# A two-layer encoder on one Trainium2 core: merged vector operations, another order of products, and another end of the last norm

## The chip, the core and the metric

The kernel runs on one core of one Trainium2 chip. Each engine has an instruction queue of its own: TensorE (PE) multiplies, VectorE (DVE), ScalarE (ACT) and GpSimd (POOL) work on rows, SyncE (SP) issues DMAs, and POOL issues some as well. The metric is the device time of one execution in microseconds. Before, the median of three runs is 1638.21 us, from 1637.58 to 1638.83.

## The reference

A trunk of two layers over 512 tokens of width 1024, all in float32. Each layer is

```python
proj = x @ w_in[i]          # q, k, v of attention; q, k, v, g of retention; two gates
ya = neighbourhood_attention(...)   # 8 heads of 64, window 8 x 16 on a 64-wide grid
yb = bidirectional_retention(...)   # 4 heads, key width 128, value width 256
merged = sigmoid(gate_a) * (ya @ w_branch_a[i]) + sigmoid(gate_b) * (yb @ w_branch_b[i])
x = layer_norm(ALPHA * x + merged @ w_out[i], ln1_g[i], ln1_b[i])
ffn = conv_glu_ffn(x, w_up[i], conv_w[i], conv_b[i], w_down[i])
ple = sigmoid(x @ w_ple_gate[i]) * (p[i] @ w_ple_proj[i])
x = layer_norm(ALPHA * x + ffn + ple, ln2_g[i], ln2_b[i])
```

`conv_glu_ffn` makes two halves of width 2816, convolves each over three neighbouring tokens, forms gelu(a) * b and multiplies by `w_down`. The output is the 512 x 1024 array after the second layer.

## The kernel before

**Numbers.** Each float32 operand of a product is held as a rounded part and a remainder: `hi` is made by ACT, `lo = raw - hi` by DVE (128x1024 per weight tile, line 842 `split`). One product is then three matmuls, high by high, high by low and low by high (`mm3`, line 1179). Large products go over 2x2 blocks with seven block products in place of eight, called `a`, `c`, `t1`, `t2`, `d`, `t3`, `t4`. Five of them take sums or differences of blocks as operands. For the down-projection these come from `s_sums` (line 2156) out of the gated halves `gg`, in four DVE instructions of 256 columns, and are then split into `sh` and `sl`.

**Tokens.** Token rows lie in four tiles of 128. `R[0]` to `R[3]` are the running sums of the output tiles; `N1` and `N2` are their column halves of 512. `into` (line 2292, and another after line 2409) adds a product from PSUM to a half of R, `stats` takes mean and variance of it (`bn`), `moments` joins these in `mv`. `rstd` is the inverse deviation, made on POOL from a `ve` of ACT.

**Order.** Nothing is issued when it is written down. `Program` records every operation (so all rows have the one line L278), and a list scheduler (`_order` line 563, `_best` line 494) puts each region in order by due times and rough costs; `_best` repeats this for `ROUNDS` rounds with random shifts from `SEED` and keeps the best. The order of PE's products within a region comes from tables: `VG` and `FILL` for the projections, the heads (R0 to R3 retention, N0 to N7 attention) and the blocks 2 to 9 between them, `PG` for the gate products, `UP_ORDER` for the up-projection of each layer in two parts (`0a` is block product `a` of unit 0, `g` the product with the embedding gate, `A0` to `A3` the affine step of the first norm of one tile, `s` a down sum), and `SUMS_AT` for the places of some sums. The last part of the last layer (plan 0) is issued as written.

**Retention head.** `qk` are the rotated queries and keys, `s` their products, `wx` the decay weights, `ta = s * wx`, `kz` the weighted keys, from which PE makes the state `st`.

**Affine step.** The first norm's output for the residual needs four multiplications of `xn` by a half of the gain (`lnh`) and two additions to R per tile.

**End.** The last block product, `t4`, is made for tile 2 and then for tile 3, 24 matmuls of 512 columns each. For each tile: add, `bn`, `mv`, then the norm. Tile 1 goes out by a DMA of POOL that adds to the bias, which an SP DMA has put into the output far earlier. Tile 0 gets gain and shift from POOL and goes out by SP. Tile 2's scaling by `rstd` is done by ACT, its shift by POOL, per half. Tile 3 is done by DVE alone: times the gain `gp`, then `rstd` and the shift `bp2`. `gp` and `bp2` are copies of gain and shift in PSUM, in halves. Inside these, the writes are

```python
def norm_b(t, R=R):
    shift_0(slice(768, 1024))
    nc.sync.dma_start(out[:P, :], R[0])
    for c in (N1, N2):
        nc.scalar.activation(R[t][:, c], R[t][:, c], AF.Copy, scale=rs[t])
        nc.gpsimd.tensor_add(R[t][:, c], R[t][:, c], b2c[:, c])
        nc.sync.dma_start(out[t * P:(t + 1) * P, c], R[t][:, c])
```

## Time and profile before

| | |
|---|---|
| median of three runs | 1638.21 us |
| profiled execution | 1637.16 us |
| its span in the trace | 1635.4 us |
| granted TensorE clock, as a share of full speed | 0.999 |
| instructions in the trace | 26401 |
| HBM traffic over the span | 327.37 MB read, 27.79 MB written |

The profile shows one execution. The span is what the trace holds from first to last instruction; the rest of the 1637.16 us lies around it. Busy time is the union of an engine's instructions. In a timeline row stand start, duration, engine, line, operation, output and inputs, and in brackets how long the engine had waited ahead of it and for whom. In a row of groups stand count, busy time, mean nanoseconds of one, and idle time ahead of them. PE's matmuls overlap a little in the records: one of 256 columns is recorded with 283 ns, and 24 in a row take 2.88 us.

### The profile page before, as it was taken

To read this page: it belongs to the slowest core of one execution; us is meant where nothing else is said; L and a number is where in the kernel's file an instruction comes from. 1 tells how busy PE (TensorE), PEld (TensorE's weight loads), DVE (VectorE), ACT (ScalarE), POOL (GpSimd) and SP (SyncE) were. 2 spreads that over 40 slices of the span, in tenths; PEclk is the share of its full clock that TensorE was granted. 3 is DMA by queue.
4 is the path that set the end of the run, shared out by engine and by line. 5 is a ranking of instruction groups with operands and counts; after the bars stand their busy time and mean duration, and the time that the engine had idled before them with its cause. 6 is when DMAs were issued, how large, how long until landed. Compare 5 with 4: busy or idle time off the path is not lost.

```text
span 1635.4 us, 26401 instructions
## 1 busy us (share of the span) xinstructions
PE 1622.0 (99%) x10005; PEld 1460.9 (89%) x10005; DVE 1390.4 (85%) x2122; ACT 1027.0 (63%) x1545; POOL 246.3 (15%) x296
## 2 busy tenths in 40 slices
PE   9999999999999999999999999999999999999997
PEld 7889999888889899899888999998888998998986
DVE  6756998678978999879998779986799699997788
ACT  6664868645577667457486458785456675574554
POOL 0210211101211112101111111210012111110113
PEclk9999999999999999999999999999999999999999
DMA  8996777868798888769687977688598988788675
GB/s 308 269 237 164 172 153 200 273 207 252 197 290 227 224 262 203 224 211 222 174 263 190 285 186 185 176 225 251 191 261 224 283 238 238 206 204 271 175 169 129
DMA packets 108032, 360.57 MB, mean 220 GB/s; under 512 B 12800, under 2 KB 14336, under 8 KB 107904
## 3 DMA queue, kind: packets, MB, share of 16 engines
q0 software_dynamic: 36432, 130.56, 41.3%
q1 hardware_dynamic: 71472, 228.31, 38.8%
q8 instruction: 79, 1.29, 0.3%
q14 instruction: 49, 0.40, 0.1%
HBM read 327.37 MB, written 27.79 MB: 217 GB/s over the span
## 4 chain that ended last, share of the span: by engine, by line
PE 84%; DVE 11%; issue 2%; DMA 2%; POOL 1%; ACT 0%; DVEq 0%; POOLq 0%; ACTq 0%
PE u L278 31%; PE v L278 17%; PE gt L278 15%; PE w L278 8%; PE gn L278 4%; DVE lo L278 3%; PE o L278 2%; DMA rawa<-in_wpack 2%; DVE xn L278 1%; PE x L278 1%; PE ns L278 1%; PE na L278 1%; DVE t L278 1%; PE pt L278 1%; DVE ga L278 1%
## 5 line engine op out<-in xcount | busy, mean ns | idle before, releaser
L278 DVE TENSOR_TENSOR lo<-rawa,hi 128x1024 fp32r<-128x1024 f32 (+1 forms) x230 | 274.2, 1198 | 56.4 <-ACT hi L278 51.7
L278 ACT CAST hi<-rawa 128x1024 fp32r<-128x1024 f32 (+1 forms) x230 | 235.7, 1035 | 119.0 <-DMA rawa<-in_wpack 76.0
L278 POOL DMA_DIRECT2D rawa<-in_wpack x159 | 139.9, 893 | 1012.9 <-DVE lo L278 779.0
L278 DVE TENSOR_TENSOR lo<-raw,hi 128x1024 fp32r<-128x1024 f32 (+1 forms) x170 | 203.7, 1204 | 11.2 <-ACT hi L278 8.7
L278 ACT CAST hi<-raw 128x1024 fp32r<-128x1024 f32 (+1 forms) x146 | 151.0, 1040 | 9.3 <-PE u L278 5.8
L278 PE MATMUL gt<-x1t,hi 128*128 128x512 f32 x448 | 138.4, 390 | 0.0
L278 PEld LDWEIGHTS gt<-x1t,hi 128*128 128x128 f32 x448 | 83.0, 188 | 16.5
L278 PE MATMUL u<-x1t,hi 128*128 128x256 f32 x480 | 87.5, 283 | 0.5 <-DVE uh L278 0.4
L278 PE MATMUL u<-xt,hi 128*128 128x256 f32 x480 | 87.4, 283 | 0.0
L278 PE MATMUL gt<-x1t,lo 128*128 128x512 f32 x224 | 87.1, 389 | 0.0
L278 PE MATMUL u<-sh,hi 128*128 128x256 f32 x304 | 86.5, 284 | 0.0
L278 PE MATMUL v<-sh,hi 128*128 128x256 f32 x304 | 86.2, 284 | 0.0
L278 PE MATMUL v<-sh,lo 128*128 128x256 f32 x304 | 86.0, 283 | 0.0
L278 PE MATMUL v<-sl,hi 128*128 128x256 f32 x304 | 86.0, 283 | 0.0
L278 PE MATMUL u<-sh,lo 128*128 128x256 f32 x304 | 86.0, 283 | 0.0
L278 PE MATMUL u<-sl,hi 128*128 128x256 f32 x304 | 86.0, 283 | 0.0
L278 PE MATMUL v<-hi,sh 128*128 128x512 f32 x216 | 84.1, 389 | 0.0
L278 PE MATMUL v<-lo,sh 128*128 128x512 f32 x216 | 84.1, 389 | 0.0
L278 PE MATMUL v<-hi,sl 128*128 128x512 f32 x216 | 84.0, 389 | 0.0
L278 ACT ACTIVATE uh<-u 128x512 f32<-128x512 f32 x69 | 41.1, 596 | 63.1 <-PE u L278 62.9
L278 PE MATMUL gt<-ybt,hi 128*128 128x512 f32 x256 | 79.6, 392 | 0.0
L278 PE MATMUL u<-lo,sh 128*128 128x512 f32 x200 | 78.0, 390 | 0.0
(311 smaller groups left out, 4966.5 us busy)
## 6 DMA issues: line engine op xcount, KB each, us to landing
raw<-in_wpack SPq DMA_DIRECT2D x166, 512.0 KB, 7.5
rawa<-in_wpack POOLq DMA_DIRECT2D x153, 512.0 KB, 7.6
rawa<-in_wpack SPq DMA_DIRECT2D x56, 512.0 KB, 6.4
rawt<-in_wpack SPq DMA_DIRECT2D x56, 512.0 KB, 7.6
rawt<-in_wpack POOLq DMA_DIRECT2D x41, 512.0 KB, 9.3
hi<-in_wpack POOLq DMA_DIRECT2D x37, 512.0 KB, 6.6
sx<-s_scr SPq DMA_DIRECT2D x32, 512.0 KB, 10.3
lo<-in_wpack POOLq DMA_DIRECT2D x13, 512.0 KB, 5.6
```

Of the source, the lines that this page charges most:

```text
L278: r = o.call(*[real(x) for x in o.a], **{k: real(v) for k, v in o.k.items()})
```

## The change

**Sums.** `s_sums` makes both first differences in one instruction, 2 x 256 wide, and the other two from them; the places of the sums in `ss` change, so `t1`, `t2` and `t3` take their operand from other places.

**Attention.** The softmax rows of 4 groups of 256 are scaled by one 1024-wide multiply with a broadcast factor, where four tensor-scalar operations of 256 stood (16 places).

**Tables.** `FILL` of both layers, `PG` of layer 0, `SUMS_AT` and `UP_ORDER` are given in another order; `SEED` is (4, 4), one random source for each layer, and `ROUNDS` 80 in place of 120. `_legal` asserts rules of the order when the program is built.

**End.** The last `t4` for tile 3 is made in two halves of 256 columns (24 matmuls each in place of 12 of the 24 of 512 columns; the second half in a bank of its own), and tile 3's statistics are taken in four quarters (`bq`). One 256-wide addition to tile 3 is done ahead of the product. Tile 0 goes out like tile 1, by POOL's adding DMA onto a bias put there early. Tile 2's first half is now scaled and shifted by DVE, its second half by ACT, then gain and shift by POOL. Tile 3's last scaling comes in 512, 256 and 256 columns with a write each.

```diff
-FILL = (tuple('... 7t4 2t4 3a R0 8c ...'.split()),
+FILL = (tuple('... 7t4 8a 2t4 3a R0 8c ...'.split()),
...
-PG = (tuple('a 0a T2 c S g 0c S S g S 1a t1 t2 0t1 0t2 0d 0t3 1t1 0t4 1c d g 1t2 1d 1t3 t3 1t4 g t4'.split()),
+PG = (tuple('a 0a T2 c S g 0c S S g S 1a t1 t2 0t1 0t2 0d 0t3 1t1 d 1c 0t4 g 1t2 t3 1d 1t3 1t4 g t4'.split()),
...
-SUMS_AT = (('1c', '0t1', 'ga1', 'ga2'), ('1c', '9a', '0t1', '0t1'))
+SUMS_AT = (('1c', '0t1', 'ga2', 'ga2'), ('1c', '9a', '0t1', '0t1'))
...
-            (tuple('0a 0t1 A0 0c A1 g A2 0t2 A3 0d 0t3 1a 0t4 1t1 1c 1t2 1d 1t3 2a ...
+            (tuple('0a 0t1 A1 g A2 0t2 A3 0d 0t3 1a A0 1t1 1c 1t2 1d 0c 0t4 1t3 2a ...
-ROUNDS = 120
+ROUNDS = 80
-SEED = 7
+SEED = (4, 4)
...
-                for g in range(4):
-                    nc.vector.tensor_scalar_mul(S[:, g * 256:(g + 1) * 256], S[:, g * 256:(g + 1) * 256], rc[:, g:g + 1])
+                S4 = S.rearrange("p (g n) -> p g n", g=4)
+                nc.vector.tensor_mul(S4, S4, _ap(rc, 0, [[1, 4], [0, 256]]))
...
-                for t in (1,):
+                for t in (0, 1):
                     nc.sync.dma_start(out[t * P:(t + 1) * P, :], ln_par[l, 3:4, :].to_broadcast([P, D]))
...
-                nc.vector.tensor_sub(ta[:, H1], g2[:, H2], g1[:, H2])
-                nc.vector.scalar_tensor_tensor(tb[:, H1], ta[:, H1], -1.0, g1[:, H1], **op)
-                nc.vector.tensor_sub(tb[:, H2], g1[:, H1], g1[:, H2])
-                nc.vector.scalar_tensor_tensor(ta[:, H2], tb[:, H1], -1.0, g2[:, H1], **op)
+                ta, tb = ss[:, 0], ss[:, 1]
+                nc.vector.tensor_sub(_ap(ss, 0, [[512, 2], [1, 256]]), _ap(g, 0, [[768, 2], [1, 256]]), _ap(g, 256, [[0, 2], [1, 256]]))
+                nc.vector.scalar_tensor_tensor(tb[:, H2], tb[:, H1], -1.0, g[:, 0, H1], **op)
+                nc.vector.scalar_tensor_tensor(ta[:, H2], tb[:, H2], -1.0, g[:, 1, H1], **op)
...
+                    if kind == "t4" and fin and last:
+                        for q, to in enumerate(halves):
+                            for p in range(n):
+                                hi, lo = w[p // 2]
+                                r = slice((p % 2) * 512 + q * 256, (p % 2) * 512 + (q + 1) * 256)
+                                mm3(to, lh(p, 0, 1), lh(p, 1, 1), hi[:, r], lo[:, r], q == 1 and p == 0, p == n - 1, q == 0)
+                            yield
...
-                    for h, c in enumerate((N1, N2)):
-                        nc.vector.scalar_tensor_tensor(R[t][:, c], R[t][:, c], rs[t], bp2[h], op0=ALU.mult, op1=ALU.add)
+                    shift(2, N2)
+                    nc.vector.scalar_tensor_tensor(R[2][:, N1], R[2][:, N1], rs[2], bp2[0], op0=ALU.mult, op1=ALU.add)
+                    nc.sync.dma_start(out[2 * P:3 * P, N1], R[2][:, N1])
+                    for a, b in ((0, 512), (512, 768), (768, 1024)):
+                        c = slice(a, b)
+                        nc.vector.scalar_tensor_tensor(R[t][:, c], R[t][:, c], rs[t], bp2[a // 512][:, a % 512:(b - 1) % 512 + 1], op0=ALU.mult, op1=ALU.add)
                         nc.sync.dma_start(out[t * P:(t + 1) * P, c], R[t][:, c])
...
-                    shift_0(slice(0, 768))
+                    send(0)
...
+                if fin and last:
+                    into(3, slice(256, 512), w[1][:, 256:])
+                    halves += [u[1][:, :256], bank("x")[:, :256]]
...
+                        if fin and last and i == 3:
+                            for q in range(2):
+                                if q:
+                                    norm_2()
+                                    next(t4)
+                                into(3, slice(q * 256, (q + 1) * 256), halves[q])
+                                quarter(q)
```

**Rows of the order.** DVE at the first retention pair of layer 0, before (`lo_1631` is the remainder of a weight tile, the two `qk` are the operands of the pair's second product `s`):

```order
L278 TENSOR_TENSOR t_226_1573<-t_226_1573,t_227_1535 128x512
L278 TENSOR_TENSOR kf_1496<-kf_1496,t_230_1569 128x512
L278 TENSOR_SCALAR wx_1596<-dist_sb,nlg 128x384
L278 TENSOR_TENSOR qk_1594<-t_226_1573,qk_1594 128x512
L278 SCALAR_TENSOR_TENSOR wx_1596<-dist_sb,lgs,wx_1596 128x384
L278 TENSOR_TENSOR lo_1631<-raw_1432,hi_1537 128x1024
L278 TENSOR_TENSOR qk_1633<-kf_1496,qk_1633 128x512
L278 TENSOR_TENSOR ta_1642<-s_1576,wx_1596 128x512
L278 TENSOR_TENSOR ta_1652<-s_1586,wx_1596 128x512
L278 SCALAR_TENSOR_TENSOR kz_1636<-kz_1598,zeta,kz_1636 128x128 x4
```

and in the changed kernel (the two `qk` are 1603 and 1631):

```order
L288 TENSOR_SCALAR wx_1583<-dist_sb,nlg 128x384
L288 TENSOR_TENSOR kf_1493<-kf_1493,t_230_1571 128x512
L288 TENSOR_TENSOR t_226_1561<-t_226_1561,t_227_1565 128x512
L288 SCALAR_TENSOR_TENSOR wx_1583<-dist_sb,lgs,wx_1583 128x384
L288 TENSOR_TENSOR qk_1603<-kf_1493,qk_1603 128x512
L288 TENSOR_TENSOR qk_1631<-t_226_1561,qk_1631 128x512
L288 TENSOR_TENSOR lo_1636<-raw_1460,hi_1567 128x1024
L288 TENSOR_TENSOR ta_1639<-s_1574,wx_1583 128x512
L288 TENSOR_TENSOR ta_1649<-s_1586,wx_1583 128x512
L288 TENSOR_TENSOR lo_1658<-rawa_1361,hi_1593 128x1024
L288 TENSOR_SCALAR wx_1695<-dist_sb,nlg 128x384
L288 SCALAR_TENSOR_TENSOR kz_1665<-kz_1596,zeta,kz_1665 128x128 x4
```

Both second `qk` stand ahead of the first `lo` now, and a second `lo` and a `wx` stand ahead of `kz`.

DVE at the up-projection of layer 1. The affine step of tile 0 (`R_13509` before, its `xn_12937`) stood ahead of that of the other tiles:

```order
L278 TENSOR_TENSOR lo_14701<-rawa_14389,hi_14694 128x1024
L278 TENSOR_TENSOR R_14323<-R_14323,u_14475 128x512
L278 TENSOR_TENSOR xn_12937<-xn_12937,lnh_14561 128x512
L278 TENSOR_TENSOR xn_12937<-xn_12937,lnh_14558 128x512
L278 TENSOR_TENSOR R_13509<-R_13509,xn_12937 128x512 x2
```

In the changed kernel tile 0 (`R_13452`, its `xn_12877`) comes last of the four, ahead of a `lo` and a sum in `uh`:

```order
L288 TENSOR_TENSOR lo_14844<-rawt_2373_14592,hi_14812 128x1024
L288 SCALAR_TENSOR_TENSOR gg_14808<-gt_14736,cw_8049,gg_14808 128x511
L288 TENSOR_TENSOR xn_12877<-xn_12877,lnh_14485 128x512
L288 SCALAR_TENSOR_TENSOR gg_14808<-gt_14736,cw_8049,gg_14808 128x511
L288 TENSOR_TENSOR xn_12877<-xn_12877,lnh_14490 128x512
L288 TENSOR_TENSOR xn_12877<-xn_12877,lnh_14495 128x512
L288 TENSOR_TENSOR xn_12877<-xn_12877,lnh_14500 128x512
L288 TENSOR_TENSOR R_13452<-R_13452,xn_12877 128x512 x2
L288 TENSOR_TENSOR lo_14910<-rawa_14563,hi_14905 128x1024
L288 TENSOR_TENSOR uh_14762<-uh_14762,v_14699 128x2x256
```

The block has gone behind the tiles 1 to 3 and stands between the convolution's `gg` steps and `uh`.

DVE at the end, from tile 2's `mv` on; before, `R_14309` is tile 2 and `R_14323` tile 3:

```order
L278 BN_AGGR mv_17038<-bn_17019 128x2
L278 SCALAR_TENSOR_TENSOR R_14309<-R_14309,mv_17038,gb_17013 128x512
L278 SCALAR_TENSOR_TENSOR R_14309<-R_14309,mv_17038,gb_17015 128x512
L278 TENSOR_TENSOR R_14323<-R_14323,u_16792 128x512
L278 BN_STATS bn_17022<-R_14323 128x6
L278 BN_AGGR mv_17068<-bn_17022 128x2
L278 SCALAR_TENSOR_TENSOR R_14323<-R_14323,mv_17068,gb_17013 128x512
L278 SCALAR_TENSOR_TENSOR R_14323<-R_14323,mv_17068,gb_17015 128x512
L278 SCALAR_TENSOR_TENSOR R_14323<-R_14323,rstd_17071,gb_16932 128x512
L278 SCALAR_TENSOR_TENSOR R_14323<-R_14323,rstd_17071,gb_16934 128x512
```

In the changed kernel `R_14249` is tile 2 and `R_14255` tile 3, `x_16957` is the second column half of the last product:

```order
L288 BN_AGGR mv_16972<-bn_16950 128x2
L288 TENSOR_TENSOR R_14255<-R_14255,u_16723 128x256
L288 BN_STATS bq<-R_14255 128x6
L288 SCALAR_TENSOR_TENSOR R_14249<-R_14249,mv_16972,gb_16944 128x512
L288 TENSOR_TENSOR R_14255<-R_14255,x_16957 128x256
L288 BN_STATS bq<-R_14255 128x6
L288 BN_AGGR mv_17013<-bq 128x2
L288 SCALAR_TENSOR_TENSOR R_14255<-R_14255,mv_17013,gb_16944 128x512
L288 SCALAR_TENSOR_TENSOR R_14255<-R_14255,mv_17013,gb_16946 128x512
L288 SCALAR_TENSOR_TENSOR R_14249<-R_14249,rstd_16977,gb_16863 128x512
L288 SCALAR_TENSOR_TENSOR R_14255<-R_14255,rstd_17016,gb_16863 128x512
L288 SCALAR_TENSOR_TENSOR R_14255<-R_14255,rstd_17016,gb_16865 128x256 x2
```

Tile 2 keeps one scaling by `mv`, between the two halves of tile 3, and gets its `rstd` behind both of tile 3's.

POOL at the end, before (tile 1 is `R_13541`, tile 0 `R_13509`):

```order
L278 TENSOR_TENSOR rstd_16978<-ve_16976,mhalf 128x1
L278 TENSOR_TENSOR R_13509<-R_13509,lng_16787 128x1024
L278 DMA out<-R_13541 128x1024
L278 TENSOR_TENSOR R_13509<-R_13509,lnb_16788 128x768
L278 TENSOR_TENSOR rstd_17041<-ve_17040,mhalf 128x1
L278 TENSOR_TENSOR R_13509<-R_13509,lnb_16788 128x256
L278 TENSOR_TENSOR R_14309<-R_14309,lnb_16788 128x512 x2
L278 TENSOR_TENSOR rstd_17071<-ve_17070,mhalf 128x1
```

and in the changed kernel (tile 1 is `R_13482`, tile 0 `R_13452`):

```order
L288 TENSOR_TENSOR rstd_16909<-ve_16907,mhalf 128x1
L288 TENSOR_TENSOR R_13452<-R_13452,lng_16718 128x1024
L288 DMA out<-R_13482 128x1024
L288 DMA out<-R_13452 128x1024
L288 TENSOR_TENSOR rstd_16977<-ve_16976,mhalf 128x1
L288 TENSOR_TENSOR R_14249<-R_14249,lng_16718 128x512
L288 TENSOR_TENSOR rstd_17016<-ve_17015,mhalf 128x1
L288 TENSOR_TENSOR R_14249<-R_14249,lnb_16719 128x512
```

Tile 0's shift is gone and its DMA is POOL's, and gain and shift of tile 2's second half stand around tile 3's `rstd`. SP wrote tile 0, tile 2 in two halves and tile 3 in two halves, in this order; now it writes tile 2's second half, its first half, and then tile 3 in 512, 256 and 256 columns.

94 lines of the change are left out of this document (53 added, 41 removed).

## The prediction

> **What bounds the kernel now.** I read the page's first lines, then PE's waits in the timeline, then the windows.
>
> ```profile
> span 1635.4 us, 26401 instructions
> PE 1622.0 (99%) x10005; PEld 1460.9 (89%) x10005; DVE 1390.4 (85%) x2122; ACT 1027.0 (63%) x1545; POOL 246.3 (15%) x296
> PE 84%; DVE 11%; issue 2%; DMA 2%; POOL 1%; ACT 0%; DVEq 0%; POOLq 0%; ACTq 0%
> ```
>
> PE is busy for 1622.0 of 1635.4 us, so all its idle time is 13.4 us. The change takes no product away: it keeps PE's work and adds 12 matmuls. More than 13.4 us can't be won, and the next rows show that far less can. They are the longer waits of PE in the timeline (start, duration, operation, then in brackets the idle time before it and its releaser).
>
> ```profile
> 166.67 0.50 PE L278 MATMUL s<-qk,qk 128*128 128x256 f32 x2 [0.47 <-ACT qk L278]
> 167.48 1.21 PE L278 MATMUL s<-qk,qk 128*128 128x256 f32 x8 [0.31 <-DVE qk L278]
> 435.18 0.47 PE L278 MATMUL u<-hi,mt 128*128 128x512 f32 x1 [1.09 <-DVE ve L278]
> 991.35 0.39 PE L278 MATMUL o<-su,qx 128*128 128x256 f32 x1 [0.39 <-DVE qx L278]
> 1400.84 0.39 PE L278 MATMUL v<-sx,lo 128*128 128x256 f32 x1 [0.27 <-DVE lo L278]
> 1409.92 0.47 PE L278 MATMUL u<-x1t,hi 128*128 128x256 f32 x2 [0.42 <-DVE uh L278]
> 1621.31 5.60 PE L278 MATMUL u<-xw,k 128*128 128x512 f32 x24
> PE warm L278 <- DVE warm L278: 1.2, 1, 1.2
> ```
>
> The last timeline row ends PE's work at 1626.91; behind it lie 1635.4 - 1626.9 = **8.5 us of tail**. That leaves 13.4 - 8.5 = 4.9 us ahead of it; 1.2 of that is the start (the row of the waits view below it), so the body holds 3.7, of which these six waits are 2.95. The kernel is thus PE's stream, a few waits for DVE, and the tail. Whether DVE has room shows in two windows (length; busy time and count of PE, PEld, DVE, ACT, POOL; clock; DMA share; GB/s).
>
> ```profile
> 520.00:680.00 160.00, 159.89 (x976) 144.02 (x975) 159.12 (x223) 103.80 (x135) 23.50 (x29) 1.00 0.80 216
> 1360.00:1480.00 120.00, 119.22 (x761) 108.64 (x760) 118.33 (x162) 73.81 (x97) 16.82 (x21) 1.00 0.81 220
> ```
>
> In the feed-forward stretches DVE is as full as PE: 1.67 us free of 120. There DVE's order decides whether PE waits; a DVE saving alone buys at most the wait that PE has there.
>
> **The DVE edits.** Durations by shape (count | busy, mean ns):
>
> ```profile
> L278 DVE TENSOR_SCALAR S<-S,rc 128x256 f32<-128x256 f32 x64 | 18.5, 348 | 0.3
> L278 DVE TENSOR_TENSOR lo<-raw,hi 128x1024 fp32r<-128x1024 f32 x166 | 200.9, 1217 | 11.2 <-ACT hi L278 8.7 <-DMA raw<-in_wpack 2.2
> L278 DVE TENSOR_TENSOR ss<-gg 128x256 f32<-128x256 f32 x44 | 17.7, 416 | 0.1
> L278 DVE TENSOR_TENSOR xn<-xn,lnh 128x512 f32<-128x512 f32 x32 | 20.6, 681 | 0.0
> ```
>
> The attention scaling had 64 instructions in 18.5 us of busy time, 18.5/16 = 1.16 per place. One 1024-wide multiply is priced by the `lo` row: 1.22. It costs 16 x 0.06 = 1 us more of DVE at most, where DVE isn't full: **zero** on the path, between -0.5 and +0.5. On this edit the page "VectorE: DVE Perf Modes" of the Trainium skill (The perf-mode tier table; The TRN2 errata) speaks against merging: in fp32 it gives a tensor-scalar operation twice the rate of a tensor-tensor one. By the formula that it gives, with half the elements counted for tensor-scalar, an estimate is 4 x (151+128)/0.96 = 1.16 us against (151+1024)/0.96 = 1.22; the two rows above agree, and neither result moves the sum.
>
> The sums: 44 instructions in 17.7 us are 0.40 each, so two of them cost 0.80 in each of 22 places; one 2x256 subtraction is as wide as the 512-wide row, 0.68. That saves 0.12 x 22 = 2.7 us of DVE in all. PE's work covers all of it except where DVE releases PE; I take -0.2, between 0 and -0.7 (the two waits after 1397 and nothing else).
>
> **The order of the body.** First retention pair of layer 0: PE waited 0.47 + 0.31 for `qk`. The second `qk` now stands ahead of a `lo` of 1.22, not behind it, so -0.78. What is late next is `kz`, which now has a second `lo` and a `wx` ahead of it.
>
> ```profile
> 168.54 1.12 DVE L278 SCALAR_TENSOR_TENSOR kz<-kz,zeta,kz 128x128 fp32r<-128x128 f32 x4
> 172.09 0.28 PE L278 MATMUL st<-vh,kz 128*128 128x256 f32 x1
> L278 DVE TENSOR_SCALAR wx<-dist_sb,nlg 128x384 f32<-128x384 f32 x8 | 3.3, 413 | 0.1
> ```
>
> It ended at 169.66, needed at 172.09: cover 2.43. From that go 1.22 + 0.41, and 0.78 because PE arrives earlier: 0.02 is left. So the gain stands only just: -0.78 to 0, and I take -0.7.
>
> At 991, `qx` moves ahead of three retention multiplies and `su` is made earlier: -0.39 to 0, taken -0.3. At 435 the row of DVE ahead of the wait is unchanged and DVE is full: 0. At 1397 to 1410, the affine block A0 (4 `xn` x 0.68 and 2 additions to R like them, 6 x 0.68 = 4.1 us in busy time) goes behind the `lo` that PE waited for. PE's own product `w` leaves the same stretch.
>
> ```profile
> 602.21 2.88 PE v L278 x24
> ```
>
> That row of the chain of waits is the price of such a product: 24 matmuls, 2.88. DVE is relieved of 4.1 and PE arrives 2.88 earlier, a net margin of +1.2 against waits of 0.27 and 0.42: -0.69 to 0, taken -0.6. Sum of named gains: -0.2 - 0.7 - 0.3 - 0.6 = **-1.8**.
>
> Everything else in the tables (FILL with `8a` ahead of `2t4 3a`, PG[0], SUMS_AT, UP_ORDER of layer 0) puts products before others whose operands the trace of before shows only in the old order. Moved products can meet late operands. Their price is between 0 and one 1024-wide split, 1.22, per place; I take half of one, **+0.6**, nearest to the waits of 0.3 to 0.5 that such orders left before. Body: **-1.2**, between -2.9 and +2.
>
> **The tail.** What runs after PE's last product:
>
> ```profile
> 1624.95 0.69 DVE L278 BATCH_NORM_STATS2 bn<-R 128x6 f32<-128x512 f32 x1
> 1626.00 1.41 DVE L278 SCALAR_TENSOR_TENSOR R<-R,mv,gb 128x512 f32<-128x512 f32 x2
> 1627.32 0.68 DVE L278 TENSOR_TENSOR R<-R,u 128x512 f32<-128x512 f32 x1
> 1628.77 0.21 DVE L278 BATCH_NORM_AGGREGATE mv<-bn 128x2 f32<-128x12 f32 x1
> 1630.67 1.41 DVE L278 SCALAR_TENSOR_TENSOR R<-R,rstd,gb 128x512 f32<-128x512 f32 x2 [0.26 <-POOL rstd L278]
> L278 DVE BATCH_NORM_STATS2 gn<-o 128x6 f32<-128x256 f32 x32 | 12.7, 420 | 1.9 <-PE o L278 1.9
> 1618.55 0.30 ACT L278 ACTIVATE nmr<-nmu,rstd 128x1 f32<-128x1 f32 x1 [0.64 <-POOL rstd L278]
> 1625.92 0.20 ACT L278 ACTIVATE ve<-mv 128x1 f32<-128x1 f32 x1 [2.05 <-DVE mv L278]
> 1626.84 1.33 ACT L278 ACTIVATE R<-R,rstd 128x512 f32<-128x512 f32 x2 [0.72 <-POOL rstd L278]
> 1623.48 0.89 POOL L278 DMA_DIRECT2D out<-R  x1
> 1627.64 2.49 POOL L278 TENSOR_TENSOR R<-R,lnb 128x512 f32<-128x512 f32 x2 [0.18 <-ACT R L278]
> 1630.09 0.55 POOL L278 TENSOR_TENSOR rstd<-ve,mhalf 128x1 f32<-128x1 f32 x1
> 1632.10 0.33 SPq L278 DMA_DIRECT2D out<-R  x1
> ```
>
> Before, tile 3's addition did not wait for PE (ended 1626.91): it ran at 1627.32, as soon as DVE was free of tile 2. **DVE is the queue, so two column halves of PE's product bring nothing by themselves**, and as 24 x 0.12 = 2.88 for half of 5.60 they put PE's end 0.1 later, still under cover.
>
> DVE up to `mv` of tile 3: one `bn` of 0.69 becomes two of 0.42, an early 256-wide addition (0.42) is new, so tile 2's `mv` comes (0.84 + 0.42 - 0.69 =) 0.5 later. Then one scaling of 0.70 of tile 2 leaves. Half of a 512-wide addition has already been done; the rest costs one addition of 0.42, its `bn`, another addition and `bn` (1.68 in all, against 0.68 + 0.69). The balance, +0.5 - 0.7 + 0.3 = +0.1, leaves tile 3's `mv` where it was, 1628.98, within 0.1. Then DVE does 2 scalings of tile 3, one of tile 2 (0.70), one of tile 3 and two of 256 (0.42 each) where it had 4 of tile 3: it ends 0.4 later, near 1632.5.
>
> POOL is longer. `mv` of tile 2 is 0.5 later and ACT makes `nmu` ahead of `ve` (0.2 more): `rstd` 1626.84 + 0.7 = 1627.5 at the latest, 1627.4 taken. ACT: `nmr` 0.3, the half row 0.7: 1628.4. POOL: gain 1.25 to 1629.7, `rstd` of tile 3 0.55 to 1630.3 (before, 1630.64, so tile 3's last scaling isn't held up by it), shift 1.25 to **1631.6**. SP's first write waits for this, and the other four stand behind it in SP's order although the data of some are ready.
>
> ```profile
> 270.23 0.33 SPq L278 DMA_DIRECT2D gb_scr<-p  x1
> 270.60 0.43 SPq L278 DMA_DIRECT2D B<-in_rpb  x1
> out<-R SPq DMA_DIRECT2D x4, 256.0 KB, 2.0
> out<-R SPq DMA_DIRECT2D x1, 512.0 KB, 2.7
> out<-R POOLq DMA_DIRECT2D x1, 512.0 KB, 5.4
> ```
>
> SP issues 0.37 apart: 1631.6 + 4 x 0.37 = 1633.1 for the last, against 1632.10: +1.0. The last write is 128 KB. From 512 KB in 2.7 and 256 KB in 2.0, 128 KB lands by the same slope after 1.65: -0.35. So the least is +0.65. But 256 KB move in 0.7 by that slope, and issues come every 0.37: the five (1 MB in all) queue at the DMA engines. By the slope the last lands at 1631.6 + (2.0 - 0.7) + 4 x 0.7 = 1635.7, against 1632.1 + 2.0 = 1634.1: +1.6. I take +1.3, between **+0.6 and +1.6**, nearer to the queue since issue is twice as fast as transfer. By the Trainium skill's page "DMA: Bandwidth & Descriptors" (Anatomy of one DMA) a transfer costs about 2.0 us and its bytes at 436 GB/s; an estimate for the 1 MB so issued is 1631.6 + 2.0 + 2.4 = 1636.0, +1.9 on the sum. The measured 2.0 for 256 KB lies under the page's 2.6, so the rows decide. Tile 0's accumulating write now follows tile 1's on POOL, at 1624.4, and lands 5.4 later, 1629.8: off the path. The second bias fill is one SP issue far from the end.
>
> **Sum.** Against the profiled execution, 1637.16 (span 1635.4 and 1.8 around it): -1.2 + 1.3 = +0.1. The median of the runs is 1638.21, 1.05 above that execution; the same sum gives **1638.3**.
>
> **The rivals.** *The waits go, and the end does what it says (faster).* All 3.7 us of idle time in the body vanish, the wait at 435 with them through DVE's savings, nothing new arises, and POOL's half of tile 2 is written early, so that the smaller last piece saves 0.35 in place of the loss: 1638.21 - 3.7 - 0.35 = 1634.2. For it: DVE releases every wait shown, and the change saves DVE 2.7 us. Against: 435 keeps its order on DVE, and `kz` is left 0.02 of cover. Chance 0.10.
>
> *A late DVE block (slower).* One affine block of 4.1 us now falls ahead of a split or a `uh` that PE needs in 1360 to 1480. It decides from the point at which PE's own work ahead of that operand is shorter than the block. At most 1.67 of it finds idle DVE time in that window, so PE waits between 4.1 - 1.67 = 2.4 and 4.1, 3.3 in the middle. With the gain of 0.6 at 1397 and the tail's +1.3: 1638.21 + 3.3 - 0.6 + 1.3 = 1642.2. For it: DVE is busy for 118.33 of 120, and A0 is put between two `gg` steps and a `uh`. Against: PE's `0c` is moved behind A0 too, 2.88 of work that PE can do meanwhile. Chance 0.15.
>
> *The end alone does what it says.* POOL's second half of tile 2 is ready before tile 3's first write, SP's order costs nothing and the last piece of 128 KB saves 0.35: 1638.21 - 1.2 - 0.35 = 1636.7. Against: by the steps above POOL ends at 1631.6, later than any of DVE's parts but the last two. Chance 0.15.
>
> **How the numbers follow.** Forecast 0.60 at 1638.3; its own range adds the ends of body (-2.9 to +2) and tail (+0.6 to +1.6): 1635.9 to 1641.8. The 0.2% that a measurement of this kernel can tell from no change is 3.3 us: 1634.9 to 1641.5. Forecast and better tail lie within, but for a corner. The range 1634.7 to 1641.6 holds both and the near edge of each outer rival; under 2 in 10 stay outside. So faster 0.11 (the rival and a corner), same 0.73, slower 0.16.
>
> **What would show it.** Right: no wait of PE for `qk` near 167; the wait near 435 as before; tile 3's `mv` within 0.2 of 2.07 after PE's end; SP's five writes in a burst right behind POOL's last addition; 9 to 10 us from PE's last matmul to the end. Wrong: a new wait of PE over 1 us in either feed-forward stretch, a wait for `kz` near 171, tile 2's second half written before tile 3's `mv`, or a DMA that PE or DVE now waits for at a product that the tables moved.

## The result, and the profile after

The changed kernel takes **1641.54 us** (median of 12 runs, 1639.5 to 1644.37) against 1637.99 for the kernel before (12 runs, 1636.29 to 1639.13). The ratio is 1.0024, with a 95% interval from 1.0017 to 1.0032: slower by 3.55 us in the medians, where 1638.3 was forecast. The profiled execution of it took 1642.68 us, 1.1 over its own median.

First, the page's opening lines for the changed kernel, and the end of PE's work in its timeline:

```profile
span 1640.7 us, 26336 instructions
PE 1623.0 (99%) x10017; PEld 1461.3 (89%) x10017; DVE 1390.6 (85%) x2057; ACT 1024.4 (62%) x1544; POOL 250.7 (15%) x295
1629.46 1.60 PE L288 MATMUL x<-xw,k 128*128 128x256 f32 x12
```

The last row is the second half of tile 3's `t4`. It has 12 matmuls, not 24, and so has the first half: 24 of 256 columns in all, in place of 12 of 512, which makes the 12 more in PE's count.

PE is recorded busy for 1.0 us more. Its last matmul now ends at 1631.06, and 1640.7 - 1631.06 = 9.64 us lie behind it (before: 8.49). So the end costs 1.15 more, and most of the rest is idle time of PE ahead of it. Here are PE's waits, grouped by what PE waited for (us in total, times, longest):

```profile
PE u L288 <- DVE uh L288: 1.9, 2, 1.1
PE w L288 <- DVE lo L288: 1.7, 1, 1.7
PE warm L288 <- DVE warm L288: 1.2, 1, 1.2
PE u L288 <- DVE ve L288: 0.8, 1, 0.8
PE w L288 <- ACT hi L288: 0.6, 1, 0.6
PE st L288 <- DVE kz L288: 0.4, 1, 0.4
```

The waits for `qk`, `qx` and the `uh` near 1410 are gone from the list. Two for `uh` (1.9), one for `lo` (1.7) and one for `hi` (0.6) have come. The timeline tells where:

```profile
167.20 0.63 PE L288 MATMUL kz<-ident,kf 128*128 128x128 f32 x4 [0.21 <-DVE ta L288]
529.91 0.28 PE L288 MATMUL u<-sh,lo 128*128 128x256 f32 x1
531.03 0.50 PE L288 MATMUL u<-x1t,hi 128*128 128x256 f32 x2 [0.84 <-DVE uh L288]
600.33 0.47 PE L288 MATMUL u<-x1t,hi 128*128 128x256 f32 x2 [1.07 <-DVE uh L288]
783.70 0.50 PE L288 MATMUL w<-hi,k 128*128 128x512 f32 x1 [0.64 <-ACT hi L288]
785.87 0.50 PE L288 MATMUL w<-lo,k 128*128 128x512 f32 x1 [1.67 <-DVE lo L288]
984.75 0.50 PE L288 MATMUL st<-vh,kz 128*128 128x256 f32 x2 [0.42 <-DVE kz L288]
```

All the new large waits lie in layer 0, in places where the prediction showed no wait: 531, 600 and 784 us. One of its own signs of being wrong has come, a new wait of over 1 us in a feed-forward stretch.

The idle time in such rows is a little short of what is lost, since PE's records overlap. A better measure is the distance from one matmul's start to the next, less what a matmul in an unbroken stream takes (0.227 us for 512 columns, 0.120 for 256, 0.109 for 128, and 0.427 for the matmuls that warm PE up). Summed by stretch of the span, in us, this gives for every profiled execution that is used below:

```
run                       520-560 560-640 770-860 860-1110 1390-1420 other    all  behind  us of that
                                                                                   last    execution
before                       0.00    0.34    0.16     0.96      1.52  5.42   8.40    8.49   1637.16
after                        1.08    1.31    2.89     1.60      0.90  4.64  12.41    9.64   1642.68
after_again_1                1.08    0.00    0.02     3.91      1.06  4.78  10.84    9.88   1641.44
after_again_2                1.06    0.01    1.27     1.09      0.91  4.71   9.05    9.67   1639.26
after_same_chip              1.08    0.01    0.74     1.16      0.80  4.67   8.44    9.89   1638.93
after_five_moved             1.07    0.39    1.60     1.91      0.74  4.94  10.65    9.65   1640.93
tile0_old_way                1.10    0.17    0.00     2.73      0.96  5.49  10.46    9.64   1640.63
load_ahead                   1.06    0.01    0.00     1.00      0.73  4.39   7.18    9.66   1637.36
body_with_old_end            1.08    0.28    0.18     1.68      0.90  4.59   8.70    8.48   1637.82
body_old_end_same_chip       1.09    0.45    1.22     0.84      0.97  5.45  10.02    8.47   1639.12
load_ahead_old_end           1.08    0.37    0.01     1.47      0.69  4.31   7.92    8.48   1637.03
t3_put_back                  0.00    1.38   -0.03     2.87      0.45  5.90  10.57    8.48   1639.32
t3_moved_alone               1.06    0.46    0.14     0.98      1.68  4.36   8.69    8.48   1637.43
end_in_old_order             0.00    0.84    0.20     1.00      1.67  5.24   8.97   10.18   1639.56
end_old_order_same_chip      0.00    0.40    0.19     1.00      1.52  5.31   8.42    9.85   1638.78
end_three_writes             0.00    1.30    0.19     1.02      1.63  4.78   8.91   10.17   1639.59
end_writes_by_readiness      0.00    0.43    0.20     1.01      1.67  4.99   8.31    9.60   1638.32
fill_alone                   1.08    0.88    0.00     0.98      0.78  5.51   9.22    8.40   1638.22
ops_in_old_order             0.01    0.97    0.38     0.97      1.67  5.94   9.95    8.94   1639.23
sums_alone                   0.01    1.11    0.43     0.98      1.67  5.25   9.44    8.61   1638.41
```

In every row, the execution's time less the columns "all" and "behind last" leaves 1620.3 to 1620.7, so these two columns hold the difference between two executions to within 0.4 us. From the first row to the second, they are 1.08 + 0.97 + 2.73 + 0.64 - 0.62 - 0.78 = +4.0 in the body and +1.15 at the end. The executions differ by 5.52; of the 0.36 left, 0.22 lies around the span (1.98 in place of 1.76).

The four executions of the unaltered changed kernel (rows 2 to 5) show two kinds of loss. The one at 531 is **constant**, 1.06 to 1.08. Those at 600, near 784 and from 860 to 1110 **come and go**: 0 to 1.31, 0.02 to 2.89, 1.09 to 3.91. The one near 600 comes and goes in before's order too: 0.34 to 1.30 over `before` and the four rows that begin with `end_`. The runs spread likewise: their standard deviation is 1.4 to 1.6 us for the changed kernel (11 or 12 runs) and 0.7 to 0.9 for the one before (11 to 33).

### The profile page after: what moved, and what is told of

The parts are those of the page before. It is cut to its first block, busy times and chain, and to the rows that moved or that the text cites. A ratio compares the mean times of both kernels' runs of the same rounds, so it can differ in the third digit from the quotient of the medians.

```text
span 1640.7 us, 26336 instructions
## 1 busy us (share of the span) xinstructions
PE 1623.0 (99%) x10017; PEld 1461.3 (89%) x10017; DVE 1390.6 (85%) x2057; ACT 1024.4 (62%) x1544; POOL 250.7 (15%) x295
## 4 chain that ended last, share of the span: by engine, by line
PE 79%; DVE 12%; issue 4%; DMA 2%; ACT 1%; POOL 0%; SPq 0%; DVEq 0%; POOLq 0%; ACTq 0%
PE u L288 28%; PE gt L288 16%; PE v L288 15%; PE w L288 8%; PE gn L288 4%; DVE lo L288 3%; PE o L288 2%; DVE xn L288 2%; DMA rawa<-in_wpack 1%; DVE R L288 1%; PE x L288 1%; PE ns L288 1%; PE na L288 1%; DVE t L288 1%; PE pt L288 1%
## 5 line engine op out<-in xcount | busy, mean ns | idle before, releaser
L288 PEld LDWEIGHTS u<-x1t,hi 128*128 128x128 f32 x480 | 75.7, 192 | 3.3 <-issue 1.2
L288 PE MATMUL u<-hi,sh 128*128 128x512 f32 x200 | 77.9, 389 | 0.0
```

Of the source, the lines that this page charges most:

```text
L288: r = o.call(*[real(x) for x in o.a], **{k: real(v) for k, v in o.k.items()})
```

## The experiments

Three theories were open: the end costs what its last writes cost (by their issue, or by their transfer); the new order makes PE wait for DVE at a few places (by the order itself, or by loads that come late); or the merged operations are dearer than they look.

Editing anything, even the end alone, makes the scheduler plan both layers anew. So in most of these kernels the order of the two layers was read from a table taken from one of the two kernels, and only what the edit names differs:

```diff
-        end, order = _best(jobs)
...
+        segs = _frozen(jobs)
```

A difference is in us against the runs of the kernel before on the same chip, mean against mean; its standard error is 0.2 to 0.6. All of these kernels compute the whole result.

**1. The merged operations alone.** Before's order, with the 1024-wide scaling and the 2x256 sums, and then with the sums alone:

```diff
-                for g in range(4):
-                    nc.vector.tensor_scalar_mul(S[:, g * 256:(g + 1) * 256], ...)
+                nc.vector.tensor_mul(S4, S4, _ap(rc, 0, [[1, 4], [0, 256]]))
...
-                nc.vector.tensor_sub(ta[:, H1], g2[:, H2], g1[:, H2])
...
+                nc.vector.tensor_sub(_ap(ss, 0, [[512, 2], [1, 256]]), ...)
```

> The kernel of before with its very order of instructions, read from a table in place of being planned anew; only the merged vector operations of the change (attention scaling, first differences of the sums) are in it. Theory A (the loss is the new order of the body and the new end; the merged operations are harmless): 1637.6 to 1638.1, that is 0 to -0.4 us against before, and the same waits of PE as before. Rival B (the merged operations themselves cost, by stalling DVE where PE waits): slower by 1.5 us or more, with new PE waits for ss, sl or S.

> The order of before with the merged first differences of the sums alone; the attention scaling as before. If the merged sums cost (a wider instruction at the place of the first narrow one delays what DVE does next): +1 us or more, with waits near 600 or 1609 as with both edits. If they don't: within 0.6 us of before.

Measured: both edits 1639.1 against 1637.12, ratio 1.0008 (0.9999 to 1.0017), mean +1.6; the sums alone 1638.08 against 1637.29, 1.0005 (0.9996 to 1.0014), mean +0.9. Neither interval excludes no change, and neither run shows a gain. With both edits the 1637.6 to 1638.1 of theory A was missed, and the mean is at the 1.5 of the rival (standard error 0.3). But the waits that the rival named, for `ss`, `sl` or `S`, did not come; with both edits, a second for `uh` and two for `lo` did:

```profile
PE u L278 <- DVE uh L278: 0.7, 2, 0.4
PE u L278 <- DVE lo L278: 0.6, 2, 0.4
```

The two profiles lost 9.95 and 9.44 in the body, where the five of before's order without the merged operations lost 8.31 to 8.97. The groups by shape in the changed kernel's profile bear out the prices:

```profile
L288 DVE TENSOR_TENSOR S<-S,rc 128x1024 f32<-128x1024 f32 x16 | 19.5, 1221 | 0.3
L288 DVE TENSOR_TENSOR ss<-gg 128x512 f32<-128x512 f32 x22 | 15.0, 683 | 0.1
```

Each scaling takes 1.22 us and each pair of differences 0.68, as predicted. (The estimate of 1.22 from the Trainium skill's page "VectorE: DVE Perf Modes", The TRN2 errata, agrees with the first row.) But the 2.7 us that they were to save DVE are not seen in its busy time: 1390.4 before, 1389.9 with the sums alone, 1391.0 with both. Two narrow differences in a row had taken less than twice one of them:

```profile
533.09 0.75 DVE L278 TENSOR_TENSOR ss<-gg 128x256 f32<-128x256 f32 x2
```

Whether the merged operations cost time in the changed order stays **open**: that order was not run with the old operations.

**2. The end alone, and the body alone.** The new end (with its second fill of the bias) in before's order; and the changed order with the old end; then both again, with the whole change, on one chip:

> The kernel of before with its very order in both layers; only the new end is in it (and the bias fill that it needs). Theory A: +1.2 us against before (from the last matmul to the end of the span 9.6 us in place of 8.5), so about 1639.2. Rival C (the new end is neutral or better, and all of the 3.5 us is lost in the body): 1637.5 to 1638.2, with 8.0 to 8.6 us behind the last matmul.

> The changed kernel in its own order in both layers (read from a table), with the end of before. Theory A (losses of the body and of the end add up): the loss of 3.5 us less the 2.0 us that the new end alone measured, so +1.5 us or a little more against before, 1638.5 to 1640, and 8.3 to 9.0 us behind the last matmul. Rival (the end's loss comes from the body's order, or the reverse): the whole +3.5 us stays, or none does.

> The changed kernel, timed on the same chip as the three below, since parts measured on different chips did not add up: +3.5 us whole, but +0.1 us for its body with the old end and +2.4 us for its end in the old order. Theory I (they add up on one chip, within 0.7 us): its loss equals that of the body alone plus that of the end alone. Theory J (the new end makes the body slower too): it is 1.5 us or more above the sum.

> The order of the changed kernel with the end of before, again. Theory I: +0.5 to +2 us against before. Theory J: 0 to +0.5 us, with a spread of its runs no wider than that of before, while that of the changed kernel is twice as wide.

> The order of before with the new end, again: +1.2 to +2.4 us by both theories; the distance from the last matmul to the end 9.6 to 10.2 us.

| | time, before | ratio (95%) | mean |
|---|---|---|---|
| end_in_old_order | 1639.56, 1637.12 | 1.0014 (1.0005 to 1.0023) | +2.2 |
| body_with_old_end | 1637.97, 1637.94 | 1.0001 (0.9992 to 1.0010) | +0.2 |
| after_same_chip | 1640.49, 1637.25 | 1.0023 (1.0014 to 1.0032) | +3.6 |
| body_old_end_same_chip | 1637.88, 1637.25 | 1.0006 (0.9997 to 1.0014) | +0.75 |
| end_old_order_same_chip | 1638.92, 1637.25 | 1.0011 (1.0002 to 1.0019) | +1.6 |

The end is slower by itself, by 1.6 to 2.2, of which its profiles show 1.4 to 1.7 behind PE's last matmul. The body is not the gain of 1.2 that was forecast but a small loss, if anything (at first +0.2, where theory A asked for +1.5 or more). On the one chip the two make 2.3 of the 3.6: 1.2 us are left that neither part shows alone. The standard error of this remainder is about 0.6, so theories I and J are not decided by it.

**3. Where the 1.2 could lie.** The new end differs from the old one in two things that happen away from it: an SP DMA that fills tile 0's rows with the bias, and tile 0's adding write on POOL.

```diff
-                for t in (1,):
+                for t in (0, 1):
                     nc.sync.dma_start(out[t * P:(t + 1) * P, :], ln_par[l, 3:4, :].to_broadcast([P, D]))
```

> The changed kernel, but tile 0 goes out as before (shift on POOL, SP write), without the second bias fill and without the second adding DMA. Theory J1 (the fill of 512 KB and the adding DMA are what disturbs the rest): 1.5 us or more less than the changed kernel. Theory K (it is the burst of five writes behind POOL): no more than 0.5 us less, and still 9.4 us or more behind the last matmul.

> The order of the changed kernel with the end of before, and only the second bias fill of 512 KB added (tile 0 is then written over it by SP as before). Theory J1 (the fill makes other transfers late): +0.8 us or more against the same kernel without it, so +1.2 to +2 us against before. Rival (the fill is one SP issue in the open, and what is missing in the sum is the spread of late operands): within 0.5 us of it, +0 to +0.9 us against before.

The whole change with tile 0 sent as before: 1640.11 against 1637.25, 1.0015 (1.0006 to 1.0024), mean +2.6, so 1.0 below the whole change beside it. The fill alone on the changed order with the old end: 1638.24 against 1637.29, 1.0007 (0.9998 to 1.0016), mean +1.1, so 0.4 to 0.9 above that order without it. Both point to the fill, and both lie within about two standard errors. The profiles show no place at which it costs: tile0_old_way lost 10.46 us in the body, more than after_same_chip did, and fill_alone 9.22, between the 8.70 and 10.02 of the same kernel without the fill. With tile 0 sent as before, 9.64 us lie behind the last matmul, as in the changed kernel. This stays **open**.

**4. The end: which of its steps costs.** First the issue order of SP (tile 2's second half behind tile 3's first), then three writes in place of five (tile 2 in one piece, tile 3 in two halves):

```diff
-                    shift(2, N2)
...
+                        if a == 512:
+                            shift(2, N2)
```

> As the kernel with only the new end, but SP's five writes stand in the order in which their data are ready: tile 2's first half, tile 3's first half, tile 2's second half (POOL's), tile 3's last two quarters. If SP's order behind POOL's last addition is what the new end costs, 0.6 to 1.0 us come back: 8.6 to 9.0 us behind the last matmul, +0.2 to +0.6 against before. If the transfers themselves (1 MB within 2 us) or their number set the end, it changes by less than 0.3 against the kernel with the plain new end.

```diff
-                    for a, b in ((0, 512), (512, 768), (768, 1024)):
...
+                    nc.sync.dma_start(out[2 * P:3 * P, :], R[2])
+                    for h, c in enumerate((N1, N2)):
```

> The order of before, the new end, but tile 2 goes out in one write of 512 KB and tile 3 in two of 256 KB: three issues of SP in place of five behind POOL's last addition. Theory F (each issue in a row costs 0.45 us on SP, and the end is the last issue plus a fixed 3.3 us, whatever its size): last issue 5.2 us after the last matmul, not 6.2 to 6.5, end after 8.5 us, time within 0.6 us of before. Rival G (the end waits for 1 MB to drain through the DMA engines): the last landing moves by less than 0.4 us, the time stays 1.5 to 2.3 us above before.

By readiness: 1639.19 against 1637.12, 1.0012 (1.0003 to 1.0021), mean +1.8. Three writes: 1638.63 against 1637.94, 1.0006 (0.9997 to 1.0015), mean +1.0. SP's rows at the end, for the changed kernel, end_in_old_order, the one by readiness and the one with three writes (the length runs from the first to the last of them):

```profile
1635.39 2.41 SPq L288 DMA_DIRECT2D out<-R  x5
```
```profile
1632.17 2.61 SPq L278 DMA_DIRECT2D out<-R  x5
```
```profile
1630.87 2.87 SPq L278 DMA_DIRECT2D out<-R  x5
```
```profile
1632.46 1.64 SPq L278 DMA_DIRECT2D out<-R  x3
```

and for the last of these kernels the DMA view (count, KB, median us from issue to landing):

```profile
out<-R SPq DMA_DIRECT2D x1, 512.0 KB, 2.7
out<-R SPq DMA_DIRECT2D x2, 256.0 KB, 3.0
```

From the first issue to the end of the span are 1640.7 - 1635.39 = 5.3 us with five writes and 1637.7 - 1632.46 = 5.2 with three. So the megabyte takes as long in three writes as in five: with three, a write of 256 KB lands 3.0 us after its issue, in place of 2.3 in the burst of five and 2.0 before, and the span ends 4.4 us after the last issue, in place of 3.4 to 3.7. That contradicts theory F, in which the end follows the last issue by a fixed 3.3. In the changed kernel the writes land 6.37, 7.11, 7.81, 8.15 and 8.50 us after PE's end, 0.70 to 0.74 apart for 256 KB and 0.34 for 128 KB; this is what a queue of transfers looks like. The run's +1.0 decides less: it lies between the two expectations, and the first issue came later in this profile (4.89 after PE's end, not 4.55).

By readiness SP begins 3.91 after PE's end, and 9.60 lie behind the last matmul. The two profiles of the same kernel with the plain new end, end_in_old_order and end_old_order_same_chip, begin at 4.55 and 4.54 and have 10.18 and 9.85. So the end comes 0.25 to 0.6 sooner, less than the 0.6 to 1.0 expected, and the runs (+1.8 against +2.2 on the same chip) do not tell it from no change. With the old end the same queue reads

```profile
1629.09 4.96 SPq L288 DMA_DIRECT2D out<-R  x5
```

Its five writes begin 0.6 us behind PE's end and are spread over 5 us, so that little is left to drain when the last is issued; now they all stand behind POOL's last addition. By the Trainium skill's page "DMA: Bandwidth & Descriptors" (Anatomy of one DMA) the estimate for the megabyte was 4.4 us to its last landing; the traces have 4.0 to 4.5 from the first issue to the last landing, and another 1.1 to 1.3 to the end of the span. The Trainium skill's page states that fit for DMAs that GpSimd issues, and these are SP's.

**5. The wait at 531.** The theory was that one product moved in `PG` makes it. Before, block `1t3` and block `1t4`, which add to the same bank of PSUM, had `t3` between them:

```diff
- ... g 1t2 1d 1t3 t3 1t4 g t4
+ ... g 1t2 t3 1d 1t3 1t4 g t4
```

Once this alone was done in the kernel before, and once it alone was undone in the changed order with the old end (layer 0 planned anew in both):

> The kernel of before with this one entry of PG changed as in the changed kernel: t3 ahead of 1d (layer 0 is planned anew with it, layer 1 keeps its order). Theory L: a wait of PE for uh of 0.7 to 1.0 us near 531 appears, and the time rises by about 1 us. Rival: no wait there above 0.3 us.

> The order of the changed kernel with the end of before, but in the table PG of layer 0 the gate product t3 stands behind 1t3 again and not ahead of 1d (layer 0 is planned anew with it, layer 1 keeps its order). Theory L (1t4 adds into the bank that 1t3 has just filled and that DVE must first read; t3 between them gave DVE 2.9 us for that): no wait of PE for uh near 531, where it was 0.84 recorded (1.0 by the spacing of matmuls), and 0.5 to 1.5 us less than the same kernel without it (+0.2 and +0.7 us against before), so -0.8 to +0.2 us against before. Rival (PE waits there because DVE is full): the wait stays or moves by less than 20 us.

t3_moved_alone: 1637.62 against 1637.29, 1.0004 (0.9995 to 1.0012), mean +0.7. Its PE and DVE rows:

```profile
529.58 0.28 PE L278 MATMUL u<-sh,lo 128*128 128x256 f32 x1
530.69 0.50 PE L278 MATMUL u<-x1t,hi 128*128 128x256 f32 x2 [0.84 <-DVE uh L278]
529.96 0.68 DVE L278 TENSOR_TENSOR uh<-uh,u 128x512 f32<-128x512 f32 x1
```

The wait is there, the same 0.84 as in the changed kernel. PE starts its last matmul of `1t3` at 529.58; DVE then reads `u` in 0.68 us (529.96 to 530.64), and PE starts `1t4` into that bank at 530.69. Before, the 24 matmuls of `t3` filled this gap; PE's first matmul of `t3`, DVE's reading of `u`, and PE's first of `1t4` were

```profile
525.41 0.40 PE L278 MATMUL u<-hi,sh 128*128 128x512 f32 x1
526.57 0.68 DVE L278 TENSOR_TENSOR uh<-uh,u 128x512 f32<-128x512 f32 x1
530.88 0.40 PE L278 MATMUL u<-x1t,hi 128*128 128x256 f32 x2
```

In t3_put_back (1637.52 against 1637.29, 1.0004, 0.9995 to 1.0013, mean +0.4) the column 520-560 is back at 0.00. The cause of this wait is **settled**, since it comes with the one edit and goes with the other; it holds PE for 1.1 us. The run times do not show that price by itself: t3_put_back was expected at -0.8 to +0.2, and the same order without it measured +0.2 and +0.75. Its profiled execution, the slowest of its eleven, lost 1.38 near 600 and 2.87 beyond 860.

**6. The waits that come and go.** Rows near 600 show a chain. DVE in the changed kernel and in after_same_chip:

```profile
592.96 2.48 DVE L288 TENSOR_TENSOR xn<-xn,lnh 128x512 f32<-128x512 f32 x4
595.37 2.49 DVE L288 TENSOR_TENSOR R<-R,xn 128x512 f32<-128x512 f32 x4
599.51 0.68 DVE L288 TENSOR_TENSOR uh<-uh,u 128x512 f32<-128x512 f32 x1
```
```profile
591.62 2.48 DVE L288 TENSOR_TENSOR xn<-xn,lnh 128x512 f32<-128x512 f32 x4
594.02 2.48 DVE L288 TENSOR_TENSOR R<-R,xn 128x512 f32<-128x512 f32 x4
598.16 0.67 DVE L288 TENSOR_TENSOR uh<-uh,u 128x512 f32<-128x512 f32 x1
```

An affine block stands ahead of `uh` in both, but only where DVE is 1.35 us later does PE wait. So rows were moved in the changed order (six in all, though the run's name says five): two `uh` and one `lo` ahead of the block's last two additions, and near 780 one `hi` of ACT and two `lo` of DVE ahead.

```diff
 DVE, near 595
-TENSOR_TENSOR R<-R,xn 128x512 x2
-TENSOR_TENSOR lo<-rawa,hi 128x1024
 TENSOR_TENSOR uh<-uh,v 128x512
 TENSOR_TENSOR uh<-uh,u 128x512
+TENSOR_TENSOR lo<-rawa,hi 128x1024
+TENSOR_TENSOR R<-R,xn 128x512 x2
```

> The changed kernel in its own order, but for six instructions: near 595 us two uh sums stand ahead of the last two additions to R (and the lo behind them ahead of these too), and at the end of layer 0's region, near 780 us, one hi (ACT) and two lo (DVE) of the first down-projection weights stand ahead of sh, cb and gg. Theory A (PE waits there because DVE's order puts work that nobody waits for ahead): the wait of 1.1 at 600 goes, those of 0.6 and 1.7 at 784 to 786 shrink to under 1.0 in all, and the time falls by 2 to 2.8 us against the changed kernel, to about 1639.2. Rival D (DVE is full, so that what is moved ahead there shows up as a wait of the same size at the next product): less than 0.8 us gained, with new PE waits within 20 us behind those places.

Measured: 1642.14 against 1637.12, 1.0030 (1.0021 to 1.0039), mean +4.7: no gain at all. In its profile the waits at 600 and 784 to 786 are gone, but new ones stand at 797 (0.8, for `lo`) and 977 (0.9, for `qk`). So moving DVE's rows bought nothing; 1.60 us were still lost from 770 to 860. Two more single executions of the unaltered changed kernel:

> The changed kernel once more, for its waits: its runs spread from 1639.5 to 1644.4 us. Theory H (the spread is in the body: operands that come just in time are late at other places in each execution): the waits at 531 and 434 come again with the same size, those at 600, 784 and 786, 906 and 979 vary by 0.5 us or more. Rival (the same waits everywhere, and a slower clock or a longer end makes the spread): all waits within 0.2 us.

> As the run before it, a third look at the same instructions: which waits of PE come in every execution, which in some.

They took 1641.44 and 1639.26; the table has where they lost. Here the cause shows some 30 us ahead of PE's wait, on ACT, which must wait in order for a weight load. The same row in the kernel before, the changed kernel and after_again_1:

```profile
749.38 1.06 ACT L278 ACTIVATE lo<-hi 128x1024 fp32r<-128x1024 f32 x1
```
```profile
754.12 1.06 ACT L288 ACTIVATE lo<-hi 128x1024 fp32r<-128x1024 f32 x1 [4.87 <-DMA hi<-in_wpack]
```
```profile
749.24 1.06 ACT L288 ACTIVATE lo<-hi 128x1024 fp32r<-128x1024 f32 x1 [1.18 <-DMA hi<-in_wpack]
```

All rows of ACT behind it are late by as much, `sh` among them, for which DVE then waits, and PE after DVE. Over eight executions with these rows in the changed order, ACT's wait and PE's loss from 770 to 860 go together: 0.91 and 0.00, 1.18 and 0.02, 1.76 and 0.00, 2.14 and 0.18, 2.69 and 0.74, 3.23 and 1.22, 3.28 and 1.27, 4.87 and 2.89. About 2 us are cover, and what goes beyond them PE loses one for one.

```profile
756.15 1.23 DVE L288 TENSOR_TENSOR sl<-ss,sh 128x1024 fp32r<-128x1024 f32 x1 [2.81 <-ACT sh L288]
```

Why is that load late? POOL's queue in the kernel before and in the changed one:

```profile
734.76 0.86 POOL L278 DMA_DIRECT2D rawa<-in_wpack  x1 [6.49 <-DVE lo L278]
737.70 0.86 POOL L278 DMA_DIRECT2D lo<-in_wpack  x1 [2.08 <-ACT lo L278]
738.23 0.88 POOL L278 DMA_DIRECT2D hi<-in_wpack  x1
```
```profile
738.72 0.86 POOL L288 DMA_DIRECT2D rawa<-in_wpack  x1 [11.15 <-DVE lo L288]
739.26 1.21 POOL L288 DMA_DIRECT2D lo<-in_wpack  x1
739.80 1.24 POOL L288 DMA_DIRECT2D hi<-in_wpack  x1
```

The load `rawa` must wait until a `lo` of DVE has read its buffer. That `lo` stands behind more of DVE's work now (it started at 733.25 before, at 737.20 in the changed kernel), and the two loads behind `rawa` wait with it, so that three loads of 512 KB start within 1.1 us of each other. The `hi` load is issued only 1.6 us later for it (739.80, not 738.23); ACT had it 14.3 us after its issue in this profile, 10.4 after it in tile0_old_way's, and before it was there when ACT needed it 11.2 after it. Why its time differs so from one execution to another stays open. The last experiment moves one row, the `hi` load, ahead of the `rawa` load, in the changed order with the old and with the new end:

```diff
 POOL, near 731
+DMA hi<-in_wpack 128x1024
 DMA rawa<-in_wpack 128x1024
 DMA lo<-in_wpack 128x1024
-DMA hi<-in_wpack 128x1024
```

> The changed kernel's order with the old end, and one row moved on POOL's queue: the load of the weight tile `hi` that ScalarE splits near 749 us is issued ahead of the load `rawa` (which waits for a subtraction on VectorE until about 738 us) instead of two places behind it. Nothing else moves. Theory: this queue position is why ScalarE stood 0.9 to 4.9 us for that load in every run of the changed order, and why TensorE then lost up to 2.9 us near 784. So the load is issued 1 to 2.5 us earlier and is first in the queue: ScalarE's wait at `lo<-hi` is 1 us or less, TensorE loses at most 0.2 us between 770 and 860, and the time is 0.2 to 0.8 us below that of the same kernel without the move (+0.2 and +0.75 over before): between -0.3 and +0.5. Rival: the load is late because all sixteen DMA engines are busy from 740 on, whatever its place; then ScalarE's wait stays above 1 us. Second rival: the load `rawa`, now behind it, is the one that comes late, and TensorE loses the same us at its tile, between 770 and 1110.

> The changed kernel, whole, with the same one row moved on POOL's queue. Theory: as in the run with the old end, ScalarE's wait near 749 is 1 us or less and TensorE loses at most 0.2 us between 770 and 860, so the time is 0.3 to 1 us below that of the changed kernel (+3.56): +2.3 to +3.2 over before, with a narrower spread between its five runs. Rivals: wait above 1 us and +3.5 (the queue's place is not the reason); or wait gone and +3.5 with the loss at other tiles.

The load is then issued 6.0 us ahead of `rawa` (737.18 in that trace) and not 1.1 behind it, and ACT doesn't wait for it in either profile (here the one with the new end):

```profile
731.22 0.54 POOL L288 DMA_DIRECT2D hi<-in_wpack  x1 [5.20 <-PE u L288]
747.61 1.06 ACT L288 ACTIVATE lo<-hi 128x1024 fp32r<-128x1024 f32 x1
```

The nine other profiles of the changed order all have that wait, 0.9 to 4.9 us. PE's loss from 770 to 860 is 0.00 and 0.01, which by itself says less, since four of the nine lost no more than 0.18. So the load's place in POOL's queue makes ACT's wait. The times are less clear: with the old end 1638.0 against 1637.46, 1.0006 (0.9997 to 1.0015), mean +1.0, which misses the -0.3 to +0.5 expected; with the new end 1639.7, 1.0015 (1.0006 to 1.0024), mean +2.3, at the low edge of what was expected and 1.3 below the changed kernel on that chip (two standard errors). The spread did not shrink (standard deviations 1.6 and 1.4): two of the eleven runs with the old end took over 1641. The profiled execution was the fastest of its eleven with the new end and the second fastest with the old, so what the longer ones lose, and where, stays **open**. The stretch from 860 to 1110, where ACT waited 2.9 to 3.6 us for `rawa` loads in after_again_1, is the first place to look; it wasn't tried.

None of the versions beats the kernel before.

## Why the prediction was wrong

**The end was right, +1.3 forecast, +1.15 to +1.4 in the four profiles (+1.6 to +2.2 in the runs of the end alone).** Tile 3's `mv` was to come within 0.2 of 2.07 us after PE's end: it came at 1632.62 - 1631.06 = 1.56, early by 0.5, because tile 2's `mv` was only 0.1 later against PE's end and not 0.5. DVE was to end 0.4 later and ended at 5.10 against 5.17, equal. POOL decides, as predicted: its last addition ends 4.3 after PE's last matmul (0.4 sooner than the forecast's 1631.6), and SP's five writes come in a burst right behind it.

```profile
1632.36 0.26 DVE L288 BATCH_NORM_AGGREGATE mv<-bq 128x2 f32<-128x24 f32 x1
1634.11 1.25 POOL L288 TENSOR_TENSOR R<-R,lnb 128x512 f32<-128x512 f32 x1
out<-R SPq DMA_DIRECT2D x3, 256.0 KB, 2.3
out<-R SPq DMA_DIRECT2D x2, 128.0 KB, 2.3
```

Of the two bounds, issue (+0.6) and queue of transfers (+1.6), the queue is the right mechanism: the writes of 128 KB land after 2.3 us, not 1.65, the writes land 0.7 apart for 256 KB as its slope says, and from first issue to last landing are 4.2 us where that bound had 4.1. With POOL 0.4 sooner, its +1.6 becomes about the +1.15 measured.

**Of the named gains of the body two came in full, and the others didn't.** The waits for `qk` at 167 went, and though `ta` is late in their place (0.21 at 167.2), the stretch from 160 to 175 loses 0.6 by spacing in every profile of the changed order where 1.28 was lost before: -0.7, as forecast. The fear for `kz` there did not come true. At 991 the wait for `qx` went and one for `kz` at 984.75 (0.42) came: 0, not -0.3. At 1397 to 1410 the gain is there in every profile of the changed order: 1.52 before, 0.69 to 1.06 after, -0.6 as forecast. The merged operations have the durations that were said; the 0 and -0.2 taken for them are not borne out, since alone in before's order they measured +1.6 and +0.9.

**The step that failed is "everything else in the tables", +0.6, "half of one 1024-wide split".** It gave a price per place, 0 to 1.22 us, and then counted one place at half of it. (The terms of the body, with one such place, add up to -3.1 to +1.7; the -2.9 to +2 stated is near that, but not their sum.) What the runs show in its place:

- 1.1 us at 531 in every execution of the changed order. The prediction listed `PG[0]` among the tables, and the diff shows `1t3 1t4` without `t3` between them. It asked only whether operands would be late, not whether a bank that PE wants to add to is still to be read.
- 0.36 us at 240 in every one of them, and 0.44 to 0.47 (once 0.73) from 440 to 520, where 0.18 was lost before. With 531 these are 1.7 us; less the gains of 0.7 and 0.6, the constant part of the body is about +0.4, near the +0.2 and +0.75 that the body alone measured.
- 0 to 2.9 us near 784 through a DMA. The prediction followed the DMA queues at the end only; POOL's queue of loads in the body was not looked at.
- 0.8 to 3.9 us from 860 to 1110, where before's order lost 0.96 to 1.02. The cause of the surplus was not tested.
- 0 to 1.3 at 600, where an affine block stands ahead of `uh`: the second rival's very mechanism, which it put in layer 1 at 1360 to 1480, where nothing came of it. But before's order lost 0.34 to 1.30 there too, so this is not shown to be a cost of the new order.

The rival's time of 1642.2 is near the measured one, but for other reasons; that is luck. The measured 1641.54 is at the upper end of the stated range, which reached so far for the sake of the rivals. The body alone measured +0.2 and +0.75 in place of -1.2; with the end's +1.6 that explains 2.3 of 3.6 on one chip, and about 1.2 has no cause that was shown. One profile (load_ahead) did lose 7.18 us in the body, 1.2 less than before, with 1.17 more behind the last matmul, which looks like the forecast's two terms. It is no support for them: it was the fastest of eleven executions, whose mean is +2.3, and the 1.06 at 531 is in it.

## What to carry to other kernels

Go through a new order of products twice: once for operands that may come late, and once for banks and buffers that may come free late; a product that adds to the bank just filled needs another between (here 1.1 us without it). Where a risk is priced per place, count the places. Compare the DMA queues of both orders too, since a load that waits for its buffer holds up all loads behind it on its queue, and its lateness shows only 30 us later and on another engine. And where a kernel's executions spread, one profile shows one draw: four of the same kernel gave 8.4 to 12.4 us of loss, and only what all four had in common could be settled from them.
